# Masks made ahead by GpSimd, one fused multiply-subtract on VectorE, and more blocks loaded whole, in a softmax-gradient kernel

One core of a Trainium2 chip. The metric is the device time of one execution in microseconds (us), median of several; lower is better.

## The reference

```python
logits: (8, 1024, 8192) float32; labels: (8, 1024) int32, 0 <= label < 8192
softmax = exp(logits - max) / sum(exp(logits - max))     # along the last axis
out = softmax - one_hot(labels)                          # float32, same shape
```

That is 8192 rows of 8192 numbers: 268 MB in, 268 MB out, and a few operations per number.

## The kernel before

128 rows, one on each partition, are a "row" `t` of the program; there are T = 64 of them. Two rows make a block `b` of 8 MB, 32 blocks. SBUF holds three blocks (`SLOTS = 3`), in which everything happens in place. A letter for each block says whether its load is one transfer ("w", whole) or two, one per row ("r").

```python
LOADS = "rrrrrwwwwwwwwwwwwwwwwwwwwwrrrrrr"      # blocks 5 to 25 whole
...
for t in range(T):
    w = run(nc.scalar, [w_max], act, "activation", out=x, in_=x, func=Act.Exp,
            bias=m[:, t : t + 1], scale=1.0, accum_out=s[:, t : t + 1])
    w_sum = run(nc.vector, [w], dve, "reciprocal", out=r[:, t : t + 1], in_=s[:, t : t + 1])
    if t + 1 < T:
        if (t + 1) % G == 0:
            load((t + 1) // G)          # waits for the stores of the block three before
        w_max = row_max(t + 1)          # VectorE, waits for the load
    if t > 0:
        store(t - 1)
    ...                                 # ScalarE: x *= r, 8192 columns
    ...                                 # VectorE: x -= (iota == label), iota in PSUM, 8192 columns
    finished.append(w)
```

`iota` holds the column numbers as int16 in PSUM. GpSimd works only at the start. Loads are issued by SyncE, stores by ScalarE's queue.

## Time and profile before

| | before |
|---|---|
| time, median of 4 runs | 1247.61 us (1247.32 to 1248.12) |
| span of the profiled execution | 1245.6 us |
| VectorE / ScalarE / GpSimd busy | 1115.9 / 919.0 / 7.4 us |
| VectorE's wait for loads, in all | 108.5 us |
| DMA share in the windows of 20 us, from 20 to 1240 us | 0.95 to 1.07 |

The prediction below reads the groups, the windows and the chain. Windows: the time from the span's start, its length, busy us and instruction count of TensorE (twice), VectorE, ScalarE and GpSimd, then the granted clock, the mean share of time in which the 16 DMA engines were busy, and GB/s. Kernel before:

```profile
1224.00:1228.00 4.00, 0.00 (x0) 0.00 (x0) 4.00 (x2) 1.47 (x1) 0.00 (x0) 1.00 1.06 459
1228.00:1236.00 8.00, 0.00 (x0) 0.00 (x0) 2.78 (x1) 0.00 (x0) 0.00 (x0) 1.00 0.98 422
```

In short windows the share scatters about 1, so neighbours are read together. The last two stores, in the timeline of the same kernel (start, duration, engine, source line, operation):

```profile
1217.78 0.34 ACTq L68 DMA_DIRECT2D out_dram<-X  x1
1230.81 0.34 ACTq L68 DMA_DIRECT2D out_dram<-X  x1
```

### The profile page before, as it was taken

The page shows a single profiled execution, that of the slowest core. Times are in us where ns is not written, and L with a number is a line of the kernel's source. Part 1 is how long each engine was busy: PE and PEld are TensorE (multiplying, and loading weights), DVE is VectorE, ACT ScalarE, POOL GpSimd, SP SyncE. Part 2 cuts the span into 40 slices and gives each one's busy share as a digit, 9 for nine tenths or more (in the row PEclk, how much of TensorE's full clock was granted, in tenths as well). Part 3 has the DMA queues.
Part 4 walks back from the last instruction along what each step waited for, and adds up shares of the span by engine and source line. Part 5 has one row for each costly group of instructions (what it writes and reads, how often), then busy time and mean ns, then how long its engine had stood idle before and what let it go on. Part 6 is the DMA issues. An engine that isn't in the chain of part 4 may idle for free.

```text
span 1245.6 us, 592 instructions
## 1 busy us (share of the span) xinstructions
PE 0.4 (0%) x2; PEld 0.3 (0%) x2; DVE 1115.9 (90%) x196; ACT 919.0 (74%) x194; POOL 7.4 (1%) x7
## 2 busy tenths in 40 slices
PE   0000000000000000000000000000000000000000
PEld 0000000000000000000000000000000000000000
DVE  4999997888988889888898888988889999999893
ACT  3888886678767787767867678777777788887772
POOL 2000000000000000000000000000000000000000
DMA  9999999999999999999999999999999999999998
GB/s 398 427 428 432 437 436 441 436 431 425 426 438 448 432 416 440 431 436 438 426 446 437 418 434 432 435 437 442 425 427 438 430 429 437 435 431 431 436 434 388
DMA packets 15460, 536.98 MB, mean 431 GB/s; under 512 B 1728, under 2 KB 1728, under 8 KB 1760
## 3 DMA queue, kind: packets, MB, share of 16 engines
q1 hardware_dynamic: 6240, 268.50, 50.0%
q10 hardware_dynamic: 9216, 268.44, 49.9%
q14 instruction: 4, 0.03, 0.0%
HBM read 268.50 MB, written 268.44 MB: 431 GB/s over the span
## 4 chain that ended last, share of the span: by engine, by line
DMA 60%; DVE 37%; ACT 1%; DVEq 0%; issue 0%; ACTq 0%; SPq 0%
DMA X<-in_logits_dram 32%; DMA out_dram<-X 28%; DVE m L68 19%; DVE X L68 18%; ACT X L68 1%; DVEq L56 0%; DVE r L68 0%; ACTq L68 0%; SPq L223 0%; SPq L56 0%
## 5 line engine op out<-in xcount | busy, mean ns | idle before, releaser
L68 DVE TENSOR_REDUCE m<-X 128x1 f32<-128x8192 f32 x64 | 555.2, 8674 | 108.5 <-DMA X<-in_logits_dram 108.5
L68 ACT ACTIVATE X<-X,m 128x8192 f32<-128x8192 f32 x64 | 455.8, 7122 | 190.2 <-DVE m L68 190.2
L68 DVE SCALAR_TENSOR_TENSOR X<-iota,lab,X 128x8192 f32<-128x8192 int16 (+1 forms) x65 | 559.6, 8611 | 4.1 <-ACT X L68 4.1
L68 ACT ACTIVATE X<-X,r 128x8192 f32<-128x8192 f32 (+1 forms) x65 | 456.0, 7016 | 115.4 <-DVE r L68 115.4
L68 ACT ACTIVATION_READ_ACCUMULATOR X<-X,m 128x1 f32 x64 | 12.0, 187 | 0.0
L68 DVE RECIPROCAL r<-s 128x1 f32<-128x1 f32 x64 | 9.8, 153 | 1.7 <-ACT X L68 1.7
L68 POOL IOTA X<- 128x8192 int16 x1 | 6.9, 6943 | 0.0
L68 DVE TENSOR_SCALAR iota<-X 128x4096 int32<-128x4096 int32 x1 | 4.4, 4428 | 0.1
L68 ACT ACT_TABLE_LOAD x1 | 1.3, 1283 | 0.9 <-SPq L56 0.9
L68 DVE COPY lab<-iota 128x64 f32<-128x64 f32 x1 | 0.2, 225 | 0.5 <-PE iota L68 0.5
L68 PE MATMUL iota<-ident,lab_f 32*128 32x32 f32 x2 | 0.4, 299 | 22.4 <-DVE lab_f L68 22.4
L68 DVE CAST lab_f<-lab_raw 32x256 f32<-32x256 int32 x1 | 0.4, 363 | 0.0
L68 PEld LDWEIGHTS iota<-ident,lab_f 32*128 32x128 f32 x2 | 0.3, 193 | 22.4 <-DVE lab_f L68 22.4
L68 POOL TENSOR_SCALAR_AFFINE_SELECT ident<-ident 32x32 f32<-32x32 f32 x1 | 0.2, 203 | 0.1
L68 POOL MEMSET ident<- 32x32 f32 x1 | 0.1, 115 | 0.5 <-SPq L56 0.5
L212 POOL MEMSET const-bfloat16-1.0<- 128x1 bf16 x1 | 0.1, 106 | 0.0
L212 POOL MEMSET const-uint8-127<- 128x1 uint8 x1 | 0.1, 106 | 0.0
L212 POOL MEMSET const-float32-0.0<- 128x1 f32 x1 | 0.1, 103 | 0.2 <-issue 0.2
L212 POOL MEMSET const-float32-1.0<- 128x1 f32 x1 | 0.1, 103 | 0.0
## 6 DMA issues: line engine op xcount, KB each, us to landing
out_dram<-X ACTq DMA_DIRECT2D x64, 4096.0 KB, 30.9
X<-in_logits_dram SPq DMA_DIRECT2D x22, 4096.0 KB, 27.5
X<-in_logits_dram SPq DMA_DIRECT2D x21, 33.2
lab_raw<-in_labels_dram SPq DMA_DIRECT2D x1, 64.0 KB, 12.3
```

Of the source, the lines that this page charges most:

```text
L68: instruction = getattr(engine, method)(**operands)
L212: nc = _bacc.Bacc("TRN2", target_bir_lowering=False, num_devices=1)
```

## The change

Its intent: take work from ScalarE and shorten a row's way. GpSimd compares column numbers with the label for the first 5120 columns of a row, ahead of time, in four instructions of 1280 columns; each uses labels shifted by its own offset, so one small table of 1280 column numbers in SBUF serves all four. VectorE then does `x*r - mask` there in one pass. ScalarE scales only the remaining 3072 columns, which VectorE finishes as before. Both maxima of a block come first, and blocks 2 to 28 are loaded whole. The set-up of labels moves into a part of X not yet in use. Smaller parts of the diff: the label load is issued from ScalarE's queue, ahead of the first load of logits; the last row is no longer scaled and finished in two halves; the last stores are waited for on SyncE; and the section that holds the program is opened with `no_gpsimd_drain=True`.

```diff
-LOADS = "rrrrrwwwwwwwwwwwwwwwwwwwwwrrrrrr"
+HOT = 5120
+CHUNK = 1280
+LOADS = "rrwwwwwwwwwwwwwwwwwwwwwwwwwwwrrr"
...
+        def row_hot(t):
+            first = [w_chunk, w_turned] if t == 0 else [w_used[t - 2]] if t > 1 else []
+            for k in range(0, HOT, CHUNK):
+                w = run(
+                    nc.gpsimd, first if k == 0 else [], pool, "tensor_scalar",
+                    out=hot[:, t % 2, k : k + CHUNK], in0=chunk_iota[:],
+                    scalar1=label(t, k), scalar2=None, op0=Alu.is_equal,
+                )
+            w_hot[t] = w
...
+            w_rest = run(
+                nc.scalar, [w_sum], act, "activation",
+                out=x[:, rest], in_=x[:, rest], func=Act.Copy, bias=0.0, scale=r[:, t : t + 1],
+            )
+            w_used[t] = run(
+                nc.vector, [w_hot[t], w_sum], dve, "scalar_tensor_tensor",
+                out=x[:, hot_cols], in0=x[:, hot_cols], scalar=r[:, t : t + 1], in1=hot[:, t % 2, :],
+                op0=Alu.mult, op1=Alu.subtract,
+            )
+            finished[t] = run(   # the rest: iota in PSUM, as before
...
+        for b in range(B):
+            load(b)
+            row_hot(b * G)
+            row_hot(b * G + 1)
+            t = b * G
+            row_max(t)
+            row_max(t + 1)
+            if t > 0:
+                store(t - 1)
+            w = row_exp(t)
+            row_finish(t, w)
+            w = row_exp(t + 1)
+            store(t)
+            row_finish(t + 1, w)
```

I call the new VectorE operation on 5120 columns "fused" and the one on 3072 "rest".

More of the change, by code (lines that the diff above doesn't have):

```diff
@@ L10 @@
 SLOTS = 3
-LOADS = "rrrrrwwwwwwwwwwwwwwwwwwwwwrrrrrr"
-STORES = "rrrrrrrrrrrrrrrrrrrrrrrrrrrrrrrr"
+HOT = 5120
+CHUNK = 1280
+LOADS = "rrwwwwwwwwwwwwwwwwwwwwwwwwwwwrrr"
 @with_exitstack
@@ L36 @@
     B = T // G
+    REST = V - HOT
     lab_bp = labels.rearrange("a b -> (a b)").rearrange("(b q) -> b q", q=G * P)
@@ L45 @@
     X = const.tile([P, SLOTS, G, V], fp32)
-    lab_raw = const.tile([B, G * P], labels.dtype)
-    lab_f = const.tile([B, G, P], fp32)
-    ident = const.tile([B, B], fp32)
-    lab = const.tile([P, G, B], fp32)
+    lab = {k: const.tile([P, G, B], fp32, name=f"lab{k}") for k in range(0, HOT, CHUNK)}
     m, s, r = (const.tile([P, T], fp32, name=n) for n in ("m", "s", "r"))
-    iota = psum.tile([P, V], i16)
+    chunk_iota = const.tile([P, CHUNK], i16)
+    hot = const.tile([P, 2, HOT], mybir.dt.uint8)
+    iota = psum.tile([P, REST], i16)
     lab_ps = iota[:].bitcast(fp32)[:, :T].rearrange("p (j b) -> p j b", j=G)
-    with tc.tile_critical():
+    early = X[:, SLOTS - 1, 0, :]
+    lab_raw = early.bitcast(labels.dtype)[:B, : G * P]
+    at = G * P * mybir.dt.size(labels.dtype) // 4
+    lab_f = early[:B, at : at + G * P].rearrange("b (p j) -> b j p", j=G)
+    ident = early[:B, at + G * P : at + G * P + B]
+    made = X[:, SLOTS - 1, G - 1, :].bitcast(i16)[:, :REST]
+    with tc.tile_critical(no_gpsimd_drain=True):
         sem = tc.alloc_semaphore
-        got = [[sem(f"got{i}{q}") for q in range(2)] for i in range(SLOTS)]
-        put = [[sem(f"put{i}{q}") for q in range(2)] for i in range(SLOTS)]
+        got = [[sem(f"got{i}{j}") for j in range(G)] for i in range(SLOTS)]
+        put = [[sem(f"put{i}{j}") for j in range(G)] for i in range(SLOTS)]
         lab_got, dve, act, pe, pool = (sem(n) for n in ("lab_got", "dve", "act", "pe", "pool"))
@@ L74, in run @@
             return counter, count[counter.name]
-        every, rows = slice(0, P), slice(0, G)
-        PIECES = {
-            "r": [(every, slice(j, j + 1)) for j in range(G)],
-            "h": [(slice(i, P, 2), rows) for i in range(2)],
-            "w": [(every, rows)],
-        }
-        def meets(a, b):
-            sets = [[set(range(*d.indices(n))) for d, n in zip(p, (P, G))] for p in (a, b)]
-            return all(x & y for x, y in zip(*sets))
-        loaded, stored, finished = {}, {}, []
@@ L91 @@
-        last_made = []
-        def load(b, behind_first=lambda: None):
-            loaded[b] = []
-            before = stored.get(b - SLOTS, last_made if b == SLOTS - 1 else [])
-            for q, piece in enumerate(PIECES[LOADS[b]]):
-                ps, js = piece
-                free = [w for other, w in before if meets(piece, other)]
-                w = run(
-                    nc.sync, free, got[b % SLOTS][q], "dma_start",
-                    out=X[ps, b % SLOTS, js, :], in_=x_b[b, ps, js, :],
-                )
-                loaded[b].append((piece, w))
-                if q == 0:
-                    behind_first()
@@ L107, in store @@
-        def store(t):
-            b, j = divmod(t, G)
-            stored.setdefault(b, [])
-            for q, piece in enumerate(PIECES[STORES[b]]):
-                ps, js = piece
-                if js.stop != j + 1:
-                    continue
-                w = run(
-                    nc.scalar, [finished[t]], put[b % SLOTS][q], "dma_start",
-                    out=o_b[b, ps, js, :], in_=X[ps, b % SLOTS, js, :],
-                )
-                stored[b].append((piece, w))
-        def row(t):
-            return X[:, t // G % SLOTS, t % G, :]
@@ L124, in row_max @@
-        def row_max(t):
-            b, j = divmod(t, G)
-            arrived = [w for piece, w in loaded[b] if meets(piece, (every, slice(j, j + 1)))]
-            return run(
-                nc.vector, arrived, dve, "tensor_reduce",
-                out=m[:, t : t + 1], in_=row(t), axis=mybir.AxisListType.X, op=Alu.max, negate=True,
-            )
-        w_raw = []
-        load(0, lambda: w_raw.append(run(nc.sync, [], lab_got, "dma_start", out=lab_raw[:], in_=lab_bp)))
-        w_max = row_max(0)
@@ L136 @@
-        w = run(nc.gpsimd, [], pool, "memset", ap=ident[:], constant=0.0)
+        w_raw = run(nc.scalar, [], lab_got, "dma_start", out=lab_raw, in_=lab_bp)
+        w = run(nc.gpsimd, [], pool, "memset", ap=ident, constant=0.0)
         w_ident = run(
             nc.gpsimd, [w], pool, "affine_select",
-            out=ident[:], in_=ident[:], compare_op=Alu.not_equal, fill=1.0,
+            out=ident, in_=ident, compare_op=Alu.not_equal, fill=1.0,
             base=0, pattern=[[-1, B]], channel_multiplier=1,
@@ L141 @@
         )
-        made = X[:, SLOTS - 1, G - 1, :].bitcast(i16)[:, :V]
         w_made = run(
-            nc.gpsimd, [], pool, "iota", out=made, pattern=[[1, V]], base=0, channel_multiplier=0
+            nc.gpsimd, [], pool, "iota",
+            out=made, pattern=[[1, REST]], base=HOT, channel_multiplier=0,
+        )
+        w_chunk = run(
+            nc.gpsimd, [], pool, "iota",
+            out=chunk_iota[:], pattern=[[1, CHUNK]], base=0, channel_multiplier=0,
         )
         step = mybir.dt.size(labels.dtype) // 4
-        lab32 = lab_raw[:].bitcast(i32).rearrange("b (p j s) -> b j p s", j=G, s=step)
@@ L149 @@
-        w_lab = run(nc.vector, w_raw, dve, "tensor_copy", out=lab_f[:], in_=lab32[:, :, :, 0])
+        lab32 = lab_raw.bitcast(i32).rearrange("b (p j s) -> b j p s", j=G, s=step)
+        w_lab = run(nc.vector, [w_raw], dve, "tensor_copy", out=lab_f, in_=lab32[:, :, :, 0])
         for j in range(G):
@@ L152 @@
                 nc.tensor, [w_ident, w_lab], pe, "transpose",
-                out=lab_ps[:, j, :], in_=lab_f[:, j, :], identity=ident[:],
+                out=lab_ps[:, j, :], in_=lab_f[:, j, :], identity=ident,
             )
-        w_turned = run(nc.vector, [w], dve, "tensor_copy", out=lab[:], in_=lab_ps)
+        for k in lab:
+            w_turned = run(
+                nc.vector, [w], dve, "tensor_scalar",
+                out=lab[k][:], in0=lab_ps, scalar1=float(k), scalar2=None, op0=Alu.subtract,
+            )
         w_iota = run(
@@ L159, with load @@
         )
-        last_made.append(((every, slice(G - 1, G)), w_iota))
-        for t in range(T):
+        loaded, stored, finished = {}, {}, {}
+        def load(b):
+            i = b % SLOTS
+            parts = [slice(0, G)] if LOADS[b] == "w" else [slice(j, j + 1) for j in range(G)]
+            for q, js in enumerate(parts):
+                rows = [b * G + j for j in range(*js.indices(G))]
+                free = [stored[t - SLOTS * G] for t in rows] if b >= SLOTS else []
+                free += [w_iota] if b == SLOTS - 1 else []
+                w = run(
+                    nc.sync, free, got[i][q], "dma_start", out=X[:, i, js, :], in_=x_b[b, :, js, :]
+                )
+                loaded.update((t, w) for t in rows)
@@ new lines, in store, with row, label @@
+        def store(t):
+            b, j = divmod(t, G)
+            i = b % SLOTS
+            stored[t] = run(
+                nc.scalar, [finished[t]], put[i][j], "dma_start", out=o_b[b, :, j, :], in_=X[:, i, j, :]
+            )
+        def row(t):
+            return X[:, t // G % SLOTS, t % G, :]
+        def label(t, less=0):
+            return lab[less][:, t % G, t // G : t // G + 1]
+        w_max, w_sum, w_hot, w_used = {}, {}, {}, {}
+        def row_hot(t):
+            first = [w_chunk, w_turned] if t == 0 else [w_used[t - 2]] if t > 1 else []
+            for k in range(0, HOT, CHUNK):
+                w = run(
+                    nc.gpsimd, first if k == 0 else [], pool, "tensor_scalar",
+                    out=hot[:, t % 2, k : k + CHUNK], in0=chunk_iota[:],
+                    scalar1=label(t, k), scalar2=None, op0=Alu.is_equal,
+                )
+            w_hot[t] = w
@@ L164, with row_max, row_exp @@
+        def row_max(t):
+            w_max[t] = run(
+                nc.vector, [loaded[t]], dve, "tensor_reduce",
+                out=m[:, t : t + 1], in_=row(t), axis=mybir.AxisListType.X, op=Alu.max, negate=True,
+            )
+        def row_exp(t):
             x = row(t)
-            label = lab[:, t % G, t // G : t // G + 1]
-            w = run(
-                nc.scalar, [w_max], act, "activation",
+            return run(
+                nc.scalar, [w_max[t]], act, "activation",
@@ L168, with row_finish @@
                 out=x, in_=x, func=Act.Exp, bias=m[:, t : t + 1], scale=1.0, accum_out=s[:, t : t + 1],
             )
-            w_sum = run(nc.vector, [w], dve, "reciprocal", out=r[:, t : t + 1], in_=s[:, t : t + 1])
-            if t + 1 < T:
-                if (t + 1) % G == 0:
-                    load((t + 1) // G)
-                w_max = row_max(t + 1)
+        def row_finish(t, w_exp):
+            x = row(t)
+            hot_cols, rest = slice(0, HOT), slice(HOT, V)
+            w_sum = run(nc.vector, [w_exp], dve, "reciprocal", out=r[:, t : t + 1], in_=s[:, t : t + 1])
+            w_rest = run(
+                nc.scalar, [w_sum], act, "activation",
+                out=x[:, rest], in_=x[:, rest], func=Act.Copy, bias=0.0, scale=r[:, t : t + 1],
+            )
+            w_used[t] = run(
+                nc.vector, [w_hot[t], w_sum], dve, "scalar_tensor_tensor",
+                out=x[:, hot_cols], in0=x[:, hot_cols], scalar=r[:, t : t + 1], in1=hot[:, t % 2, :],
+                op0=Alu.mult, op1=Alu.subtract,
+            )
+            finished[t] = run(
+                nc.vector, [w_rest], dve, "scalar_tensor_tensor",
+                out=x[:, rest], in0=iota[:], scalar=label(t), in1=x[:, rest],
+                op0=Alu.is_equal, op1=Alu.subtract, reverse1=True,
+            )
@@ L175 @@
+        for b in range(B):
[5 more added lines that the diff above has]
+            row_max(t + 1)
             if t > 0:
                 store(t - 1)
-            n = 1 if t + 1 < T else 2
-            cols = [slice(i * V // n, (i + 1) * V // n) for i in range(n)]
-            scaled = [
-                run(
-                    nc.scalar, [w_sum], act, "activation",
-                    out=x[:, c], in_=x[:, c], func=Act.Copy, bias=0.0, scale=r[:, t : t + 1],
-                )
-                for c in cols
-            ]
@@ L187 @@
-            for c, w in zip(cols, scaled):
-                w = run(
-                    nc.vector, [w], dve, "scalar_tensor_tensor",
-                    out=x[:, c], in0=iota[:, c], scalar=label, in1=x[:, c],
-                    op0=Alu.is_equal, op1=Alu.subtract, reverse1=True,
-                )
-            finished.append(w)
+            w = row_exp(t)
[3 more added lines that the diff above has]
+            row_finish(t + 1, w)
         store(T - 1)
-        for b in range(B - SLOTS, B):
-            for _, w in stored[b]:
-                nc.scalar.wait_ge(*w)
+        for t in range(T - SLOTS * G, T):
+            nc.sync.wait_ge(*stored[t])
```

## The prediction

> **What bounds the kernel now.** I read the busy shares first, then the slices, then the queues, then the windows of 20 us, and only then the groups and the chain, because the chain alone would mislead here.
>
> The page, busy shares, slices and traffic:
>
> ```profile
> PE 0.4 (0%) x2; PEld 0.3 (0%) x2; DVE 1115.9 (90%) x196; ACT 919.0 (74%) x194; POOL 7.4 (1%) x7
> DMA  9999999999999999999999999999999999999998
> HBM read 268.50 MB, written 268.44 MB: 431 GB/s over the span
> ```
>
> VectorE at 90% looks like a bound, but the DMA row shows 90% or more in 39 of 40 slices. A digit 9 cannot tell 92% from 100%, so I asked for windows:
>
> ```profile
> 40.00:60.00 20.00, 0.00 (x0) 0.00 (x0) 20.00 (x4) 17.03 (x4) 0.00 (x0) 1.00 1.00 418
> 600.00:620.00 20.00, 0.00 (x0) 0.00 (x0) 15.70 (x4) 17.02 (x4) 0.00 (x0) 1.00 1.01 436
> 1220.00:1240.00 20.00, 0.00 (x0) 0.00 (x0) 8.88 (x2) 5.47 (x2) 0.00 (x0) 1.00 1.02 439
> ```
>
> The next to last column is the DMA share: about 1.00 in the ramp, the middle and the tail. In the packet records the first data packet starts 2.0 us into the span and the last ends at 1244.1; between them 536.9 MB move at 432 GB/s, and the packet times add up to 1.00 of 16 engines. There is no hole to fill: an engine made faster can't shorten this, and only an engine made slower can lengthen it.
>
> The compute groups (busy us, mean ns), then VectorE's largest idle time:
>
> ```profile
> L68 DVE TENSOR_REDUCE m<-X 128x1 f32<-128x8192 f32 x64 | 555.2, 8674 | 108.5 <-DMA X<-in_logits_dram 108.5
> L68 DVE SCALAR_TENSOR_TENSOR X<-iota,lab,X 128x8192 f32<-128x8192 int16 x63 | 550.7, 8742 | 0.0
> L68 ACT ACTIVATE X<-X,r 128x8192 f32<-128x8192 f32 x63 | 448.7, 7122 | 113.6 <-DVE r L68 113.6
> L68 DVE SCALAR_TENSOR_TENSOR X<-iota,lab,X 128x4096 f32<-128x4096 int16 x2 | 8.9, 4480 | 4.1 <-ACT X L68 4.1
> L68 ACT ACTIVATE X<-X,r 128x4096 f32<-128x4096 f32 x2 | 7.3, 3700 | 1.8 <-DVE r L68 1.8
> L68 POOL IOTA X<- 128x8192 int16 x1 | 6.9, 6943 | 0.0
> DVE m L68 <- DMA X<-in_logits_dram: 108.5, 26, 13.4
> ```
>
> VectorE waits 108.5 us in total for loads: that is its slack, and the two forms of each operation give a cost per column, used below. The chain's repeating unit is 77.4 us for two blocks (133.34 to 210.71): one store of 26.6, one load of 33.4, one maximum and one subtraction. That is 38.7 us a block. A 32 KB packet takes 1213 ns (median of the packet records), a row of 4 MB is 8 packets on each of 16 engines, 9.70 us, and a block of two rows in and out is 4 x 9.70 = 38.8. The period is thus the transfer time itself; the chain's passage through VectorE only says which wait happened to end last.
>
> **What the Trainium skill says.** (1) "DMA: Bandwidth & Descriptors", Specifications, gives a fabric ceiling of 435 GB/s for the 16 engines; the trace's 432 to 434 agrees. (The HBM limit of about 358 in that table does not bind in this trace.) (2) "VectorE: DVE Perf Modes", The perf-mode tier table: a two-tensor fp32 operation runs at 1x, one column a cycle at 0.96 GHz. The trace agrees: (8742 - 4480) / 4096 = 1.041 ns a column. So I expect the fused multiply and subtract to cost per column what today's compare and subtract costs. (3) "SBUF — State Buffer", Who interferes with whom: a VectorE instruction with two SBUF inputs contends with a GpSimd instruction that reads SBUF, and the second one to come is blocked for the whole instruction. The trace before can't show it: today's subtraction has one input in PSUM and GpSimd works only at the start. The new 5120-column operation has both inputs in SBUF, and the new compare reads SBUF. (4) "GPSIMD Engine Reference", Performance versus the Vector engine: 1.03 cycles a column for simple bodies, about 1.8 for a good loop in general, 2.6 with two inputs, at 1.2 GHz. The trace has only the IOTA: 6943 ns for 8192, 1.02 cycles. No trace here has the compare.
>
> **The change part by part.** Costs by line: VectorE's two-tensor operation has a fixed 0.22 us and 1.041 ns a column, so 5120 columns take 5.55 and 3072 take 3.42; back to back each costs some 0.08 less (the chain steps by 8.66 for a record of 8.74), 5.47 and 3.34. ScalarE: (7122 - 3700) / 4096 = 0.835 ns a column, fixed 0.28, so the scaling of 3072 columns takes 2.85.
>
> *ScalarE* loses 7.12 - 2.85 = 4.27 us a row, 273 us of its 919 in all, none of it on the path. *VectorE* keeps its work: 5.47 + 3.34 against 8.66, 0.15 a row more, 10 us in all. *GpSimd* gains 256 compares of 1280 columns; estimated from the skill's rates plus 0.1 us for the start (the 32-column memset took 115 ns), 1.2 us at 1.03 cycles, 2.0 at 1.8, 2.9 at 2.6; thus 310 to 740 us in all, below the span in each case.
>
> *Order.* Both maxima of a block now come first. From the start of the first: maxima end at 17.2, reciprocal 17.3, fused operation of row one to 22.8, rest to 26.1. ScalarE scales row one's rest from 17.3 to 20.2 and then has its second exponential, 7.12 + 0.19, to 27.5; VectorE stands 1.4 us. Reciprocal to 27.65, fused operation of row two to 33.1, rest to 36.45. So VectorE needs 36.5 us a block plus any wait d for GpSimd's port, against 38.7 of transfers. Today it needs 2 x 17.31 = 34.6.
>
> *Port.* GpSimd may begin the compares for the next block's row one when the buffer is freed at 22.8, and VectorE wants the port again at 27.65. Four compares have 4.85 us, 1.2 each. At 1.2 there is no wait; at 2.0 the third is still running, until 28.8, and d = 1.2 if VectorE comes next, or 3.2 if GpSimd keeps the port for its fourth. The other four compares start at 33.1 and have over 20 us beside operations with one SBUF input: no conflict.
>
> *How much d is free.* Row 0 lands at 13.4, row 1 some 9.7 later, and block 0 ends near 51. Then 31 x 36.5 = 1130 gives 1181, the last store with its latency 12, and the 3.5 from the last packet to the measured time: about 1196. So 32 d may be 51 us, d = 1.6, before VectorE sets the end in place of DMA.
>
> *Loads.* Six blocks more are loaded whole. A 64 KB packet takes 2418 ns (median), so a block in is 8 x 2.418 = 19.34 against 16 x 1.213 = 19.41: 0.06 us each, 0.4 us in all. Such a load must wait for both stores of its slot, which costs nothing while stores are queued. The closest place is the start: loads 0 to 2 and stores 0 and 1 keep DMA busy until 2 + 58.2 + 19.4 = 80, and store 2 comes at 51 + 27.5 = 78.5 plus its issue. A hole of 0 to 2 us is possible there, once.
>
> *Ramp and tail.* Labels and column numbers are ready before row 0 lands, which takes some 6 us from VectorE's start; DMA is full with loads then, so nothing comes of it. In the tail from the last row's landing: maximum 8.7, reciprocal, ScalarE's rest 2.85, exponential 7.3, reciprocal, fused 5.5, rest 3.3, 28 us against 30.4 before (1200.40 to 1230.81). DMA still had 43.7 us of stores to do at that point, so this too is hidden.
>
> Sum: 1247.6 - 0.4 for packets, -0.2 as a guess for a lighter start, and 0 for the rest: 1247.0, with no hole and d below 1.6.
>
> **Rivals.** (a) *The port makes VectorE the bound.* For it: a two-input operation, an unmeasured compare rate, only 2.2 us of slack a block. Against it: chunks keep a single hold short. Time is about 1196 + 32 d: d = 2 makes 1260, d = 3.2 makes 1298, 4% slower. (b) *The shorter path feeds DMA better.* Rows are stored without waiting for the next block's landing, which the 108.5 us of waits might suggest is worth much. Against it: the DMA share is 1.00 already, so at most the 0.7 us lost in the slow first packets, and the end, 1245 or so. (c) *Whole loads starve DMA* by freeing slots later: the start's hole, or one in each rotation. Against the latter: 21 blocks load whole now at a share of 1.00; 1248 to 1251.
>
> **Range and chances.** Three quarters for full DMA, 1245 to 1249; a tenth for small holes up to 1256; the remainder for rival (a), of which about half passes 1272. Faster by 2% would need 1223, a rate of 441 GB/s over the whole span, which no long stretch of this trace has.
>
> **What would show it.** Right: DMA share 1.00 in every window, ScalarE near 650 us busy (64 x 10.16), VectorE still near 1125 with idle time put down to loads, block period 38.7. The fused operation should read 5.5 us; if it reads longer when a compare overlaps, or VectorE idles before it, d is the excess. Wrong: DMA share below 0.98 in the middle, VectorE's waits for loads near zero, and a period of 39 or more, which is rival (a) if compares took over 1.6 us; holes only near 80 us would be rival (c).

## The result, and the profile after

| | before | after |
|---|---|---|
| time, median of 4 runs | 1247.61 us | 1251.31 us (1250.49 to 1252.12) |
| ratio, 95% interval | 1 | 1.0029 (1.0012 to 1.0047) |
| span of the profiled execution | 1245.6 us | 1248.7 us |
| VectorE's wait for loads, in all | 108.5 us | 12.0 us |
| last VectorE operation ends | 1230.8 us | 1236.0 us |

Ratios here and below are the mean time of one kernel's fast runs over that of the other's of the same rounds, so not quite the ratio of the medians quoted.

The change is the same within 2%, as predicted, and 3.7 us slower where 0.6 faster was the centre. It lies outside the 1245 to 1249 us to which the prediction gave three quarters, in the stretch up to 1256 for small holes, which got a tenth. The page of the changed kernel, busy shares and groups:

```profile
PE 0.4 (0%) x2; PEld 0.3 (0%) x2; DVE 1185.7 (95%) x262; ACT 642.3 (51%) x193; POOL 1133.4 (91%) x264
L78 POOL TENSOR_SCALAR hot<-chunk_iota,lab 128x1280 uint8<-128x1280 int16 x256 | 1129.1, 4418 | 82.9 <-DVE X L78 81.4
L78 DVE TENSOR_REDUCE m<-X 128x1 f32<-128x8192 f32 x64 | 552.7, 8675 | 12.1 <-DMA X<-in_logits_dram 12.0
L78 DVE SCALAR_TENSOR_TENSOR X<-X,r,hot 128x5120 f32<-128x5120 f32 x64 | 411.8, 6434 | 2.3
L78 DVE SCALAR_TENSOR_TENSOR X<-iota,lab,X 128x3072 f32<-128x3072 int16 x64 | 218.1, 3409 | 0.0
```

GpSimd is busy for 91% of the span, and the fused operation takes 6434 ns in the mean where 5.55 us were worked out. A mean hides its spread; the view of the mask tile gives minimum, median and maximum:

```profile
L78 POOL TENSOR_SCALAR hot<-chunk_iota,lab x256: 3506/3510/8772, 6.6 to 1213.7; 128x1280 uint8<-128x1280 int16 x128
L78 DVE SCALAR_TENSOR_TENSOR X<-X,r,hot x64: 5550/5988/8415, 31.9 to 1227.1; 128x5120 f32<-128x5120 f32 x64
```

Undisturbed, a compare takes 3.51 us and the fused operation 5.55. The rest is waiting inside the record for the port, the shared access to SBUF of the prediction's point (3), and the timeline of one block shows who waits for whom (changed kernel):

```profile
600.40 5.55 DVE L78 SCALAR_TENSOR_TENSOR X<-X,r,hot 128x5120 f32<-128x5120 f32 x1
600.66 23.95 POOL L78 TENSOR_SCALAR hot<-chunk_iota,lab 128x1280 uint8<-128x1280 int16 x4
605.87 3.41 DVE L78 SCALAR_TENSOR_TENSOR X<-iota,lab,X 128x3072 f32<-128x3072 int16 x1
610.39 0.16 DVE L78 RECIPROCAL r<-s 128x1 f32<-128x1 f32 x1 [1.11 <-ACT X L78]
610.59 7.14 DVE L78 SCALAR_TENSOR_TENSOR X<-X,r,hot 128x5120 f32<-128x5120 f32 x1
617.65 3.40 DVE L78 SCALAR_TENSOR_TENSOR X<-iota,lab,X 128x3072 f32<-128x3072 int16 x1
```

The four compares merged into one line begin at 600.66, 609.33, 612.83 and 621.11 and last 8.67, 3.51, 8.29 and 3.51 us. Counted in program order, the first is the last quarter of row two's mask, and only the second begins the next block's. The first comes just after the fused operation of row one has the port: it is held until that ends at 605.9 and then takes its 3.5. The second is under way when VectorE wants the port at 610.59; VectorE gets it some 1.59 us later (7.14 less 5.55), and the third compare, although queued, is held in turn. So d, the wait per block, is 1.59 us here, and it repeats: in blocks 1 to 16, counted from 0, every row two is at 7.14, and these blocks follow each other at 37.95 us. In blocks 17 to 20 row one is stretched as well or instead (8.41 at most), and in 21 to 30 row two takes 7.36 or 7.37. Over all rows the stretch is 56.6 us (411.8 less 64 x 5.55), 1.77 a block.

GpSimd's own round, its work for one block, is as long: 8 x 3.51 = 28.1, and 5.16 and 4.78 of being held (8.67 and 8.29 less 3.51), 38.0 in all. It has no pause there (the fifth figure with a count is GpSimd's busy time):

```profile
620.00:660.00 40.00, 0.00 (x0) 0.00 (x0) 38.66 (x10) 20.03 (x6) 40.00 (x10) 1.00 1.01 434
```

VectorE at 37.95, GpSimd at 38.0 and transfers at 38.7 thus lie within 2% of each other.

Transfers stay full through the middle: 1.00 and 433 GB/s from 100 to 1220 us, as before from 200 to 980. What the windows show of a loss is at the end. Windows of the changed kernel, to set against those of before:

```profile
1224.00:1228.00 4.00, 0.00 (x0) 0.00 (x0) 2.85 (x3) 3.77 (x3) 0.00 (x0) 1.00 0.71 303
1228.00:1236.00 8.00, 0.00 (x0) 0.00 (x0) 7.96 (x2) 1.94 (x1) 0.00 (x0) 1.00 0.92 397
1236.00:1238.00 2.00, 0.00 (x0) 0.00 (x0) 0.00 (x0) 0.00 (x0) 0.00 (x0) 1.00 0.61 262
```

and its last maxima (two merged) and last two stores in the timeline:

```profile
1199.53 17.26 DVE L78 TENSOR_REDUCE m<-X 128x1 f32<-128x8192 f32 x2
...
1225.80 0.34 ACTq L78 DMA_DIRECT2D out_dram<-X  x1
...
1236.00 0.34 ACTq L78 DMA_DIRECT2D out_dram<-X  x1
```

The last block's maxima wait for no load: VectorE simply comes to them late. Store 62 is issued at 1225.8 in place of 1217.8 and store 63 at 1236.0 in place of 1230.8, and DMA runs dry before the packets of each. Summed from the packet records (by how much the packets in flight fall short of 16), 2.5 us are missing between 1220 and 1240; in the kernel before, nothing is. Not all of that is loss. The kernel before lacks 0.94 us after 1240, where some of the 16 engines finish before others, and the changed kernel 0.08. From the first packet to the last it is 1.24 us before and 2.57 after: 1.3 us of the 3.1 by which the profiled spans differ. The first packet is another 0.47 us later in this profile, and the records of the packets add up to 0.95 us more (1244.57 and 1245.52 us on each engine, in the mean).

### The profile page after: what moved, and what is told of

Its sections match the earlier page's. It is cut to its first block, busy times and chain, and to the rows that moved or that the text cites. A ratio compares the mean times of both kernels' runs of the same rounds, so it can differ in the third digit from the quotient of the medians.

```text
span 1248.7 us, 978 instructions
## 1 busy us (share of the span) xinstructions
PE 0.4 (0%) x2; PEld 0.3 (0%) x2; DVE 1185.7 (95%) x262; ACT 642.3 (51%) x193; POOL 1133.4 (91%) x264
## 4 chain that ended last, share of the span: by engine, by line
DVE 49%; DMA 26%; ACT 15%; POOL 5%; issue 3%; SPq 0%
DVE m L78 27%; DVE X L78 21%; ACT X L78 15%; DMA out_dram<-X 14%; DMA X<-in_logits_dram 12%; POOL hot L78 5%; DVE r L78 1%; SPq L78 0%; SPq L238 0%; SPq L66 0%
## 5 line engine op out<-in xcount | busy, mean ns | idle before, releaser
L78 POOL TENSOR_SCALAR hot<-chunk_iota,lab 128x1280 uint8<-128x1280 int16 x256 | 1129.1, 4418 | 82.9 <-DVE X L78 81.4
L78 DVE SCALAR_TENSOR_TENSOR X<-X,r,hot 128x5120 f32<-128x5120 f32 x64 | 411.8, 6434 | 2.3
L78 DVE SCALAR_TENSOR_TENSOR X<-iota,lab,X 128x3072 f32<-128x3072 int16 x64 | 218.1, 3409 | 0.0
L78 ACT ACTIVATE X<-X,r 128x3072 f32<-128x3072 f32 x64 | 182.7, 2855 | 60.6 <-DVE r L78 60.6
L78 POOL IOTA X<- 128x3072 int16 x1 | 2.7, 2677 | 0.0
## 6 DMA issues: line engine op xcount, KB each, us to landing
out_dram<-X ACTq DMA_DIRECT2D x64, 4096.0 KB, 38.2
```

The lines of the kernel that those rows point to most:

```text
L78: instruction = getattr(engine, method)(**operands)
```

## The experiments

Two theories to begin with. **P, the port**: the wait for GpSimd makes VectorE late. **L, whole loads**: the coarser loads cost the time. A third, **S**: the label load now goes ahead of the first load of logits (first data packet at 2.43 us in place of 1.96). Each run is compared with the kernel before on the same chip; five rounds unless said.

| run | masks | loads | median us | ratio (95%) |
|---|---|---|---|---|
| after_again | as changed | whole 2 to 28 | 1251.86 | 1.0032 (1.0020 to 1.0045) |
| no_compare | none in the loop | whole 2 to 28 | 1249.77 | 1.0016 (1.0003 to 1.0028) |
| old_loads | as changed | of before | 1248.56 | 1.0007 (0.9993 to 1.0021) |
| nocmp_old_loads | none in the loop | of before | 1248.58 | 1.0004 (0.9990 to 1.0017) |
| gated | kept off the port | whole 2 to 28 | 1250.13 | 1.0019 (1.0007 to 1.0032) |
| gated_old_loads | kept off the port | of before | 1248.94 | 1.0008 (0.9996 to 1.0021) |
| before_whole | kernel before | whole 2 to 28 | 1252.46 | 1.0036 (1.0024 to 1.0049) |
| late_rows | as changed | whole 2 to 25 | 1250.87 | 1.0027 (1.0013 to 1.0040) |
| early_rows | as changed | whole 5 to 28 | 1249.94 | 1.0017 (1.0005 to 1.0030) |
| labels_second | as changed | whole 2 to 28 | 1253.89 | 1.0053 (1.0041 to 1.0066) |
| chunk640 | 8 of 640 columns | whole 2 to 28 | 1251.83 | 1.0030 (1.0017 to 1.0043) |
| write_only | memset only | whole 2 to 28 | 1251.27 (one run, state unknown) | none |

The medians of before beside these were 1247.48, 1247.83 and 1247.87 us.

### The changed kernel again

> The changed kernel as it is, on the chip of the next three runs. All theories: 1.002 to 1.004 of the kernel before (1250 to 1252 us), with the fused operation of a block's second row stretched by the same wait for GpSimd's port and a short hole in the transfers near 1220 us.

As expected. Its first data packet is at 1.94 us, as before the change, and the time is no better: the late first packet of the first profile was a matter of that execution. The hole is again 2.5 us between 1220 and 1240. So S is not what makes the difference.

### No compares in the loop

```diff
         def row_hot(t):
+            if t > 1:
+                w_hot[t] = w_hot[t - 2]
+                return
```

> GpSimd compares for the first two rows only and every later row uses those masks again (a wrong result on purpose). Theory P, the port: all fused operations after the first blocks take 5.55 us, VectorE's block falls from 37.95 to 36.4 us, it waits over 50 us in total for loads again, the hole near 1220 us is gone and the time is 1247.5 to 1249.5, 2 us or more under the changed kernel. Theory L, whole loads: the time stays within 0.7 us of the changed kernel, since the loads are the same. Theory S, the start: also unchanged.

A wrong result, on purpose. The group of the fused operation, the wait for loads (total us, times, longest) and a window of this kernel:

```profile
L78 DVE SCALAR_TENSOR_TENSOR X<-X,r,hot 128x5120 f32<-128x5120 f32 x64 | 356.2, 5566 | 2.3
```

```profile
DVE m L78 <- DMA X<-in_logits_dram: 54.2, 24, 2.9
```

```profile
1224.00:1228.00 4.00, 0.00 (x0) 0.00 (x0) 4.00 (x2) 0.95 (x1) 0.00 (x0) 1.00 1.04 451
```

The stretch, the scarcity of waits and the hole near 1224 are gone together; the early blocks follow each other at 36.4 us and VectorE ends at 1231.0. Its five times (1248.57 to 1250.20) lie wholly below those of the changed kernel (1251.06 to 1251.92), though the intervals overlap a little. Theory P holds for about 2 us, with a median 0.3 above its range; 2 more remain above the kernel before. How the gain comes about is less plain than the vanished hole suggests: this kernel lacks 1.99 us after 1240, where the engines finish unevenly, so its shortage is 2.27 us in all against 2.99 in after_again.

### The load pattern of before

```diff
-LOADS = "rrwwwwwwwwwwwwwwwwwwwwwwwwwwwrrr"
+LOADS = "rrrrrwwwwwwwwwwwwwwwwwwwwwrrrrrr"
```

> The changed kernel with the load pattern of the kernel before (blocks 5 to 25 whole in place of 2 to 28). Theory L, the coarser loads cost the time: 1248 to 1249. Theory P: within 0.7 us of the changed kernel, that is 1250.5 to 1252.

Theory P expected no difference here and was wrong: 3.3 us come back though the compares and their stretch are all there. Theory L holds as well: the slowest of these five runs, 1250.60, is still below the fastest of the changed kernel, 1251.06. One warning: the profile fell on this kernel's slowest run (1250.60; the others 1247.76 to 1248.86), so that profile doesn't show what the typical run does.

### Labels behind the first load

```diff
-        w_raw = run(nc.scalar, [], lab_got, "dma_start", out=lab_raw, in_=lab_bp)   # first of all
+        w_raw = run(nc.scalar, [w_ident], lab_got, "dma_start", out=lab_raw, in_=lab_bp)
```

> The label load is held on the ScalarE queue until GpSimd has made the identity (about 1.3 us), so that the first load of logits goes ahead of it. Theory S, the label load delays the first packet: first packet near 1.96 us in place of 2.43 and about 0.5 us off the time. Theories P and L: no difference beyond that; VectorE's blocks stay at 37.95 us.

A miss: 2 us slower than the changed kernel, and theory S falls. The first packet is at 1.93, but the labels arrive at 10.0 us in place of 4.9, so that masks and first rows come later, and a hole opens at the start. The same window of this kernel and then of the changed one:

```profile
80.00:84.00 4.00, 0.00 (x0) 0.00 (x0) 2.85 (x3) 3.77 (x3) 4.00 (x2) 1.00 0.46 197
```

```profile
80.00:84.00 4.00, 0.00 (x0) 0.00 (x0) 4.00 (x1) 2.15 (x1) 4.00 (x2) 1.00 1.14 492
```

Store 2 is issued at 82.6 us here and at 78.0 in the changed kernel. The prediction put the moment at which DMA runs dry at 80.

### The kernel before with whole loads

The same edit of LOADS, made to the kernel before, the other way round.

> The kernel before with only the load pattern changed to whole blocks 2 to 28. Theory L, whole loads cost something by themselves: 1248.5 to 1250. Theory P: 1247.0 to 1248, since VectorE has slack there; the prediction's own term for the packets says 0.4 us less than the kernel before.

Theory L by itself: 4.6 us slower, above the range that I gave, the largest effect of all, and more than the whole change. Two windows of this kernel:

```profile
80.00:84.00 4.00, 0.00 (x0) 0.00 (x0) 4.00 (x3) 2.17 (x2) 0.00 (x0) 1.00 0.70 295
1236.00:1240.00 4.00, 0.00 (x0) 0.00 (x0) 1.74 (x1) 0.00 (x0) 0.00 (x0) 1.00 0.64 270
```

At the start the whole load of block 3 must wait for both stores of block 0 (it is issued at 81.8 us), store 2 is issued at 81.5, and until their packets start no packet is in flight from 81.43 to about 82.3; 1.25 us are missing between 70 and 100. At the end, block 28 lands whole, its first maximum starts at 1086.2, and from there VectorE goes block after block without a pause (next at 1120.8, 1155.4, 1190.1) and ends at 1237.7, so the last store is late. In the kernel before, block 28 comes row by row, its first maximum is at 1071.6, and the end is at 1230.8.

### Both parts away

> No compares after the first two rows and the load pattern of the kernel before (wrong result on purpose). If the port and the whole loads each cost their part: 1246.8 to 1248, the time of the kernel before. If what old_loads won was only the same late end of VectorE seen from the other side: the time of no_compare, 1249 to 1250.

The edits of no_compare and old_loads together. 1248.58, 0.75 us over before with 1 inside the interval: the time of the kernel before or nearly, though between the two ranges that I gave. But with the loads of before, taking away the compares wins nothing (1.0007 against 1.0004), while with whole loads it wins 2 us. The two parts don't add. That each costs where the other has used up the slack is my reading; no run shows it by itself.

### Compares kept off the port

```diff
-HOT = 5120
-CHUNK = 1280
+HOT = 4480
+CHUNK = 1120
...
             for k in range(0, HOT, CHUNK):
+                if t > 1 and t % G == 0 and k == 2 * CHUNK:
+                    first = [w_used[t - 1]]
                 w = run(
-                    nc.gpsimd, first if k == 0 else [], pool, "tensor_scalar",
+                    nc.gpsimd, first if k in (0, 2 * CHUNK) else [], pool, "tensor_scalar",
```

Two compares fit between the fused operations of a block; the others wait until the second is through.

> A right result: 4480 columns in compares of 1120, and the third and fourth compare of a block's first row wait until VectorE's fused operation of the block before is through, so that GpSimd is off the port whenever VectorE wants it. Theory P: fused operations all near 4.88 us with no stretch, VectorE's block near 37.0 us, no hole near 1220 us, and the time of no_compare, 1248.5 to 1250. Rival, GpSimd itself is too slow now that it waits: the fused operation waits for its masks and the time is over 1252.

> The gated kernel with the load pattern of the kernel before, the best candidate. Additive parts: 1246.8 to 1248, as the kernel before or 0.5 us under it. Not additive: as gated.

The tile view of gated:

```profile
L78 POOL TENSOR_SCALAR hot<-chunk_iota,lab x256: 3112/3114/3122, 9.1 to 1208.3; 128x1120 uint8<-128x1120 int16 x128
L78 DVE SCALAR_TENSOR_TENSOR X<-X,r,hot x64: 4883/4925/6496, 32.0 to 1224.7; 128x4480 f32<-128x4480 f32 x64
```

No compare is stretched now (maximum 3122 ns), the fused operation by 0.09 us at most after the first block, VectorE's early blocks follow at 37.0 us, the hole between 1220 and 1240 shrinks to 0.2 us, and the time is that of no_compare within the noise, 0.1 us over the range that I gave. The result is right and GpSimd does 87.5% of its former columns, so this speaks for the wait and against GpSimd's work as the cost. It isn't a clean separation: the split of columns changed too, GpSimd now pauses 407.5 us in all, and the interval overlaps that of the changed kernel, which was timed on another chip. With the loads of before the same mechanism gives 1248.94, again between the two ranges, at best equal to the kernel before. No version beat it.

### Where the loads cost

> The changed kernel with only blocks 26 to 28 loaded row by row again. Theory E, the end: the last whole-loaded block gives VectorE both rows only when the second has landed (near 1085 us), and from there VectorE needs its own pace to the end, so that the last stores come late; then this gets what old_loads got, 1248 to 1249.5, 2 us or more under the changed kernel. Rival, the loss is at the start (a hole near 80 us) or spread over all whole loads: 1250.5 to 1252.

> The changed kernel with only blocks 2 to 4 loaded row by row again. Theory E: no difference from the changed kernel, 1250.5 to 1252. Rival, the start: 1248 to 1249.5.

Only the letters of blocks 26 to 28, or only those of 2 to 4, were set back to "r". Theory E fails here: late_rows stays with the changed kernel. Its profile says why. Block 28's first maximum starts at 1085.1 us, as in the changed kernel at 1085.0, because VectorE with its port wait (38.2 us a block there) is itself no earlier; a row that lands sooner finds nobody free. Without the wait the earlier rows are used: 1078.0 in nocmp_old_loads against 1085.4 in no_compare, 1080.4 against 1085.7 in the gated pair. early_rows is about 1.5 us better than the changed kernel, between both ranges, with overlapping intervals and on another occasion. How the 3.3 us of old_loads divide between start and end stays open: neither half alone gives them. The two profiles of the changed kernel lack at most 0.2 us near 80, but both fell on the fastest of their runs, or on a tie for it.

### Memsets in place of compares

```diff
-        first = ... [w_used[t - 2]] if t > 1 else []
+        first = ... [w_used[t - 2], sums[t - 1 - t % G]] if t > 1 else []   # starts with the fused operation
-                    nc.gpsimd, ..., pool, "tensor_scalar", out=hot[...], in0=chunk_iota[:], ...
+                    nc.gpsimd, ..., pool, "memset", ap=hot[:, t % 2, k : k + CHUNK], constant=0.0,
```

> GpSimd only writes the masks (memset to zero, wrong result on purpose), four of 1280 columns a row, and all of them wait for the reciprocal of a block's second row so that they begin together with its fused operation. If a GpSimd instruction that reads no SBUF leaves VectorE's two-input operation alone, as the skill's SBUF page says: the fused operation stays at 5.55 us under the memsets and those keep about 1.1 us each. If the port is shared by any GpSimd work: the fused operation is stretched by up to 1.1 us, or memsets by up to 5.5. Time 1248.5 to 1250.5, as no_compare.

Wrong result on purpose. Timeline of this kernel:

```profile
649.04 5.55 DVE L78 SCALAR_TENSOR_TENSOR X<-X,r,hot 128x5120 f32<-128x5120 f32 x1
649.06 4.49 POOL L78 MEMSET hot<- 128x1280 uint8 x4 [28.79 <-DVE r L78]
```

Four memsets run fully under the fused operation, and neither they nor it are stretched, in all 31 blocks. So it is GpSimd's reading that collides and not its writing, as the page that the prediction names has it. The single time, 1251.27, is above the range that I gave and isn't explained; it is one run. Its VectorE ends at 1232.0 and nothing is missing between 1220 and 1240 (2.74 us are after 1240), so a time like the changed kernel's can come without that hole.

### Smaller compares

```diff
-CHUNK = 1280
+CHUNK = 640
```

> Eight compares of 640 columns a row in place of four of 1280. If a compare costs by the column (3.51 us for 1280): 1.75 to 1.9 us each, the wait for the port is at most one of those and VectorE's block falls below 37.95 us if the wait is under 1.59; time 1249.5 to 1251.5. If most of the 3.51 us is a fixed cost: over 2.5 us each, GpSimd then needs over 40 us a block, VectorE waits for masks and the time is over 1300.

A compare now takes 1.875 us, so the cost goes by the column: (3.51 - 1.875) / 640 = 2.55 ns, with 0.24 us fixed. The stretch shrinks to 0.27 and 0.46 us, yet the time doesn't improve (1251.83, just over my range). The chain by line and a fused operation of this kernel:

```profile
by line: POOL hot L78 97.5%; DVE X L78 0.7%; DMA X<-in_labels_dram 0.5%; DVE lab L78 0.1%; PE iota L78 0.0%; issue 0.0%; ACTq L238 0.0%; DVEq L77 0.0%; SPq L66 0.0%
```

```profile
614.01 6.01 DVE L78 SCALAR_TENSOR_TENSOR X<-X,r,hot 128x5120 f32<-128x5120 f32 x1 [1.23 <-POOL hot L78]
```

The wait has changed its place: VectorE now waits 1.23 us before the operation, for the mask itself. GpSimd's round is 16 x 1.875 + 2 x 4.14 = 38.3 us by its records, and the blocks follow at 38.0: GpSimd is the bound beside the transfers. This was hidden in the changed kernel, where its round is 38.0 too.

## Why the prediction was right, and where its steps failed

**Right.** Transfers bound the kernel, an offloaded engine couldn't shorten it, and the time stayed within 2%. The errors below are far smaller than that margin, 25 us, so "the same" would have come out of a poorer account too. The durations held: fused 5.55, rest 3.41, ScalarE's rest 2.86, ScalarE 642 us busy; VectorE's block without the wait is 36.4 (no_compare) against 36.5. On the port, VectorE goes ahead of the next queued compare, the better of the two cases worked out. Of the signs named, DMA was at 1.00 through the middle, but VectorE was busy 1185.7 us and not near 1125, and its 12.0 us of waits for loads are near the zero named for rival (a).

**The compare's term was mis-sized.** It was put at 1.2 to 2.9 us; it takes 3.51. With that, the same working says that the second compare runs from 26.3 to 29.8 and d = 2.2. Measured were 1.59 in blocks 1 to 16 and 1.82 in 21 to 30, where the two compares fall as worked out; VectorE gets the port 0.66 us before the compare's record ends. In blocks 1 to 16 the order was another: the other four compares, which were to be done long before the next fused operation, spilled over it, so that the first compare after it is still row two's.

**The port's wait used up its limit.** The prediction held 32 d = 51 us free. The stretch is 56.6 us, and the prediction's own 1196 + 32 d then gives 1252.6, near the 1251.3 measured: VectorE sets the end. That agreement is in part luck. At 37.95 us a block VectorE would have ended near 51 + 31 x 37.95 = 1228, early enough to stay hidden behind the transfers. From block 16 on it also waited 5.9 us for loads (the other 6.1 fall in block 0) and longer for the port, could not make that up, and ended at 1236.0; where row one is stretched, a part takes the place of its 1.1 us pause for ScalarE. A rule that takes the later of two bounds leaves such waits for loads out. The tail's term failed too: it counted 28 us from the last landing, while the last load packet ended at 1199.9 and VectorE 36 us later, because it still had the whole last block to do, maxima included.

**The loads' term had the wrong sign.** They were to win 0.4 us by larger packets. In the kernel before they cost 4.6 us, in the changed one about 3.3. Rival (c) had named the mechanism, slots freed later, and the place at 80 us; the packets' gain doesn't show (64 KB packets average 2430 ns in after_again against 2422 before). What the prediction missed is that a whole load also holds back the first row of its block, which VectorE needs early when it is nearly the bound.

**Where the 3.7 us are.** About 2 of them go with the port wait, and about 3.3 with the loads; they overlap, and with both taken away 0.5 to 0.75 us are left, not clear of zero; so the smaller parts of the diff show no clear cost either. What the changed kernel's profile shows directly is the hole of 2.5 us at the end, worth 1.3 us net. How the runs without the hole save their time, and why no_compare keeps 2 us, stays open.

## What to carry to other kernels

When transfers fill every window, ask of a change only what it may delay, and compare the rounds of all engines with the transfers': three at 38.0, 37.95 and 38.7 us leave nothing for a wait. Before one engine prepares data for another, measure the preparing instruction alone, and place it where its reads don't meet a two-input operation. Fewer, larger loads save little when the queue is full, and they deliver the first part late.

## What the Trainium skill lacked or had wrong

- "GPSIMD Engine Reference", Engine selection, calls one-input operations "roughly line-rate". The compare of int16 with a scalar into uint8 takes 2.55 ns a column, 3.1 cycles at the page's 1.2 GHz (3.51 us for 1280 columns, 1.875 for 640); the page has no figure for this instruction. A memset of 1280 bytes a partition takes 1.16 us.
- "SBUF — State Buffer", Who interferes with whom, says who blocks once one instruction has the port, not who is next. In the changed kernel's profile VectorE, arriving during a compare, always went ahead of the queued one, and it got the port about 0.66 us before the compare's record ended (612.18 against 612.84).
- "Perfetto Trace Analysis", GPSIMD Engine Instruction, calls GpSimd's spans unreliable. Here they were steady (minimum 3506, median 3510 ns; back to back they also start 3.5 us apart), and what the wait for the port adds is inside the record on both engines: 8.67 for 3.51 us on GpSimd, 7.14 for 5.55 on VectorE. Here the minimum is the compare's own cost, and the mean (4418) is not.
- "SBUF — State Buffer", Summary: rules for kernel authors, advises one DMA and not several for a transfer-bound load. Where buffers are reused row by row, one transfer for two rows in place of two took 1.0036 of the time (before_whole).
